# One constant in an expert stage: the order with late combinations lasts to the ninth group of experts, where it lasted to the fourth

## The chip, the cores and the metric

The kernel runs on one core of a Trainium2 chip. The metric is the device time of one execution in microseconds (us), the median over the runs. The core's engines are TensorE (PE in the profile, with its weight loads as PEld), VectorE (DVE), ScalarE (ACT), GpSimd (POOL) and SyncE (SP); SP issues nearly all DMAs.

## What is computed

Two transformer blocks in a row over 512 tokens of width 1024: attention and a feed-forward layer, then a gated linear attention and a layer of experts. The change is in the layer of experts. There are 64 experts in 8 groups of 8; each token goes to 2 experts of one group. Cut to what matters:

```python
def hier_moe(h, w_group, w_expert, w1, w3, w2):
    g_sel = jnp.argmax(g_logits, axis=-1)
    ...
    top_p, top_i = lax.top_k(e_prob, MOE_TOPK)
    gates = g_w[:, None] * top_p / jnp.sum(top_p, axis=-1, keepdims=True)
    ...
    def expert_block(args):
        xb, e = args
        hid = jax.nn.silu(xb @ w1[e]) * (xb @ w3[e])
        return hid @ w2[e]
    ys = lax.map(expert_block, (xs, block_e)).reshape(n_slots, dm)
    ys = ys * slot_gate[:, None].astype(ys.dtype)
    out = jnp.zeros((n_tok + 1, dm), ys.dtype).at[slot_tok].add(ys)[:n_tok]
```

The result is added to the residual and normalized.

## The kernel before, in words

The program is one stream per engine, written out in Python order; nothing reorders it later. After attention, feed-forward and gated linear attention (lines up to about 1000), `experts()` (L1234) does the layer of experts in 16 groups (Q = 16) of four experts, each expert with room for 32 tokens, so that a group is one tile of 128 rows. For group q:

- `choose(q)` (L1252) makes a 0/1 matrix on VectorE, four pairs of operations (L1258, L1260), that says which token sits in which of the 128 rows.
- `gather(half)` (L1263) multiplies it with the tokens on TensorE, 16 products (L1269, 32 records in the trace), and ScalarE copies the result from PSUM in four pieces (L1272). Each half is 512 of the 1024 columns.
- The first products (L1359) multiply the gathered rows with w1 and w3 in two halves (`kind` 0 and 1), each 16 products with 32 columns of weights, 32 records per run in the chain.
- `slots()` (L1274) makes three scalars per row by eight small products (L1280) and a copy on VectorE (L1282).
- ScalarE's SiLU (L1370) and VectorE's product (L1371) give the hidden tile, TensorE transposes it (L1379), ScalarE copies it (L1380).
- `second(q, hs)` (L1293) multiplies with w2 for each half of the columns (L1303); ScalarE scales the result by the gates (L1305), VectorE keeps the remainder (L1308).
- `combine(q, b, hs)` (L1285) sends the rows back to their tokens with two products (L1287, L1288) into a PSUM bank, and VectorE adds it to the accumulator (L1289). `combine_all` does this for four blocks of tokens and two halves: 16 products and 8 adds. The banks are of the tile name `mm`, three of them, which the first products use too.

The order of these steps depends on LEAD (L1329), compared with q at each place. For q <= LEAD, here groups 0 to 3, TensorE's order is: first products of half 0; gather(1) of the same group; first products of half 1; slots; the combinations of group q-1 (`after_slots`, L1339, called at L1373 behind the hidden product, with choose(q+1) ahead of the combinations on VectorE); transposes; second products; gather(0) of the next group. For q > LEAD it is: first products of half 0; slots, with choose(q+1) on VectorE (L1368); first products of half 1; transposes; gather(0) and gather(1) of the next group (L1389, L1390); second products; the combinations of group q itself (L1402). Group LEAD itself does both: the early order, and at its end gather(0), gather(1) and its own combinations. Group 15 has an ending of its own (L1403 and on), with `last_start` (L1425), the final norm and the output.

The weights come through a ring of 20 tiles of 1024 KB in SBUF, made of several pools (`ring_tile`, L1218); twelve tiles serve a group: four for each half of w1 and w3, four for w2. `ring_load` (L1175) issues loads on SP's queue in the order of use: four behind each half of the first products and four behind the second products of every group. A load waits until the products that read the slot's former tile are done; SP's queue is in order, so the loads behind it wait as well. The ring is filled ahead of the stage.

Of the kernel before, what the change touches and what calls it, by code (L numbers as in the profile page):

```python
# [97 lines left out]
class Net:  # L98
# [1135 lines left out]
    def experts(self):  # L1234
# [17 lines left out]
        def choose(q):  # L1252

            s0, s1 = (later[:, q // per - 1, x] if q >= per else self.slot[x] for x in range(2))
            at = iota[:, q % per * P:(q % per + 1) * P]
            for b in range(NB + 1):
                if b < NB:
                    nc.vector.tensor_scalar(oh[:, 0, b], at, s0[:, b:b + 1], None, op0=OP.is_equal)  # L1258
                if b:
                    nc.vector.scalar_tensor_tensor(oh[:, 1, b - 1], at, s1[:, b - 1:b], oh[:, 0, b - 1],  # L1260
                                                   op0=OP.is_equal, op1=OP.add)

        def gather(half):  # L1263

            p = pp.tile([P, NB, P], F32, name="tp", bufs=2)
            k0 = 4 * half
            for b in range(NB):
                for k in range(4):
                    nc.tensor.matmul(p[:, k], self.xt[:, b, (k0 + k) * P:(k0 + k + 1) * P], oh[:, 1, b],  # L1269
                                     start=(b + k == 0), stop=(b == NB - 1), skip_group_check=True)  # L1270
            for k in range(4):
                nc.scalar.activation(xs[:, k0 + k], p[:, k], AF.Copy, scale=self.vec(V_FN2, k0 + k))  # L1272
# [50 lines left out]
        def combine_all(q):  # L1323
            for b in range(NB):
                for hs in halves:
                    combine(q, b, hs)


        LEAD = 3  # L1329
        choose(0)  # L1330
        gather(0)
        next(route)
# [6 lines left out]
        def after_slots(q):  # L1339
            nonlocal tail  # L1340
            if q + 1 < Q:
                choose(q + 1)
            if 0 < q <= LEAD:
                combine_all(q - 1)
            if q + 1 == Q:
                self.last_start()
                tail = start_tail()

        tail = None
        for q in range(Q):  # L1350
            ps = pp.tile([P, 2 * EF], F32, name="mm", bufs=3)
            for kind in range(2):
                if kind and q <= LEAD:
                    gather(1)
# [7 lines left out]
                self.ring_load(4 if q or not kind else 3)  # L1362
                if kind == (q <= LEAD):
                    if q:
                        sv = slots()
                    sc, sg, st = (sv[:, c:c + 1] for c in range(3))
                    if q > LEAD:
                        after_slots(q)  # L1368
            hid = self.rp.tile([P, EF], F32, name="tmp")
            nc.scalar.activation(hid, ps[:, :EF], AF.Silu, scale=sc)  # L1370
            nc.vector.scalar_tensor_tensor(hid, ps[:, EF:], sc, hid, op0=OP.mult, op1=OP.mult)  # L1371
            if q <= LEAD:
                after_slots(q)  # L1373
# [12 lines left out]
            if q + 1 == Q:  # L1386
                break
            if q > LEAD:
                gather(0)  # L1389
# [241 lines left out]
```

## Time and profile before

| what | us |
|---|---|
| median of 3 runs (1430.21 to 1431.56) | 1430.35 |
| the profiled execution, its own time | 1429.98 |
| its span, first to last instruction | 1428.3 |
| busy in the span: PE / PEld | 1354.5 / 1020.4 |
| busy in the span: DVE / ACT / POOL | 739.4 / 542.7 / 118.9 |
| mean granted clock of TensorE | 0.987 |

How to read it: times of the trace are counted from the span's start. "Busy" is the time in which an engine had an instruction under way. The granted clock is 1.00 at 2.4 GHz and 0.50 at 1.2 GHz. In the page's 40 slices each slice is 35.7 us; a digit is a share in tenths, and GB/s is what the DMAs moved. In the chain of waits a line is start, length and what the chain ran through. In a list of waits a line is who waited, "<-" for what, us in total, times, and (where it stands) the longest. In a table of stretches the columns are: from and to; length; busy us (and instructions) of PE, PEld, DVE, ACT and POOL; granted clock; share of the DMA engines' time; GB/s. In the order of time a line is start, length, engine, line, operation, output and inputs, and in square brackets the idle time before it and what ended it. Lines of TensorE's products and weight loads name their output and inputs by tile: `mm`, `tp`, `py` are PSUM, `h` is the pool's name for the gathered rows, the 0/1 matrix and the scaled output.

### The profile page before, as it was taken

Reading aid. Unit: us, or ns where it says so; the run is one execution under the profiler, and the core shown is the slowest. Engines: PE = TensorE matmul, PEld = TensorE weight load, DVE = VectorE, ACT = ScalarE, POOL = GpSimd, SP = SyncE. Lnnn points to the kernel's source line nnn. Section 1 sums busy time; section 2 is a strip of 40 time slices with the busy share of each in tenths; the row PEclk is TensorE's granted clock in tenths of the full one; section 3 lists DMA queues with packets and bytes.
Section 4 is the critical chain, followed back from the end, with each engine's and each line's share of the span. In section 5 each row is a group of like instructions: output and inputs, shape, how many; then the busy total and the mean of one; then the engine's idle time right before and its main releaser. Section 6 shows DMA issues by size and latency. Waiting matters only on the chain.

```text
span 1428.3 us, 20196 instructions
## 1 busy us (share of the span) xinstructions
PE 1354.5 (95%) x8266; PEld 1020.4 (71%) x8266; DVE 739.4 (52%) x1321; ACT 542.7 (38%) x980; POOL 118.9 (8%) x111
## 2 busy tenths in 40 slices
PE   7899999999999999999999999999889999999985
PEld 6688888887888888888887888875456556556542
DVE  6877788775554433444555675552332432432423
ACT  6666666764423212233443354422112112111114
POOL 2101111101100000000322122000000000000001
PEclk9999999999999999999999999999989999999997
DMA  4111111113332322232222123798998999999994
GB/s 181 32 59 60 60 60 60 60 60 120 117 108 89 118 89 89 90 116 89 89 89 79 69 90 117 285 388 323 412 407 357 420 420 421 420 419 421 420 420 179
DMA packets 42495, 282.22 MB, mean 198 GB/s; under 512 B 4864, under 2 KB 5120, under 8 KB 9504
## 3 DMA queue, kind: packets, MB, share of 16 engines
q1 hardware_dynamic: 41616, 280.05, 49.6%
q8 instruction: 66, 1.08, 0.3%
q10 hardware_dynamic: 784, 0.85, 0.2%
q14 instruction: 29, 0.24, 0.0%
HBM read 278.72 MB, written 2.10 MB: 197 GB/s over the span
## 4 chain that ended last, share of the span: by engine, by line
PE 82%; DVE 8%; ACT 4%; DMA 3%; POOL 1%; issue 1%; ACTq 0%; SPq 0%; POOLq 0%; DVEq 0%
PE mm L205 22%; PE mm L331 9%; PE tp L1269 8%; PE py L205 8%; PE tp L205 8%; PE mm L1359 7%; PE py L1303 4%; DMA wring<-in_w_dram 3%; PE mm L773 2%; PE mm L1287 2%; PE tp L1280 2%; PE mm L1288 2%; PE plog L529 1%; POOL sql L392 1%; DVE whl L178 1%
## 5 line engine op out<-in xcount | busy, mean ns | idle before, releaser
L178 DVE TENSOR_TENSOR whl<-wraw,whl 128x1024 fp32r<-128x1024 f32 x138 | 180.9, 1311 | 97.7 <-ACT whl L168 97.4
L168 ACT ACTIVATE whl<-wraw 128x1024 fp32r<-128x1024 f32 x138 | 144.5, 1050 | 102.1 <-PE mm L205 44.2
L331 PE MATMUL mm<-xh,whl 128*128 128x264 f32 (+1 forms) x736 | 181.8, 331 | 0.6 <-DVE whl L178 0.6
L205 PE MATMUL mm<-xh,whl 128*128 128x512 f32 x544 | 175.9, 397 | 0.0
L331 PEld LDWEIGHTS mm<-xh,whl 128*128 128x128 f32 x736 | 119.8, 189 | 15.1 <-issue 3.4
L1269 PEld LDWEIGHTS tp<-h,xt 128*128 128x128 f32 x1024 | 115.9, 192 | 7.8 <-issue 3.4
L1269 PE MATMUL tp<-h,xt 128*128 128x128 f32 x1024 | 118.5, 276 | 0.3 <-DVE h L1260 0.3
L205 PEld LDWEIGHTS mm<-xh,whl 128*128 128x128 f32 x544 | 102.2, 188 | 23.2 <-issue 2.3
L205 PE MATMUL mm<-xl,whl 128*128 128x512 f32 x272 | 106.0, 390 | 0.0
L331 PE MATMUL mm<-xl,whl 128*128 128x264 f32 (+1 forms) x368 | 99.5, 323 | 0.0
L1359 PE MATMUL mm<-wring,h 128*32 128x512 f32 x664 | 96.1, 595 | 3.4 <-ACT h L1272 2.0
L1308 DVE SCALAR_TENSOR_TENSOR h<-py,sv,h 128x512 fp32r<-128x512 f32 (+1 forms) x33 | 24.2, 735 | 137.0 <-ACT h L1305 136.9
L205 PE MATMUL mm<-ogh,whl 128*128 128x512 f32 x256 | 83.6, 396 | 1.5 <-ACT ogh L536 1.5
L1289 DVE TENSOR_TENSOR acc<-acc,mm 128x512 f32<-128x512 f32 (+1 forms) x120 | 73.8, 673 | 8.0 <-PE mm L1288 7.7
L1272 ACT ACTIVATE h<-tp,vecs 128x128 f32<-128x128 f32 x128 | 36.5, 368 | 104.9 <-PE tp L1269 104.9
L1370 ACT ACTIVATE tmp<-mm,sv 128x256 f32<-128x256 f32 x16 | 7.6, 474 | 178.7 <-PE mm L1359 163.6
L1287 PE MATMUL mm<-h,ss 128*128 128x512 f32 (+1 forms) x128 | 61.7, 483 | 9.0 <-DVE acc L1289 5.2
L205 PE MATMUL py<-xh,whl 128*128 128x512 f32 x208 | 65.8, 391 | 0.0
L205 PE MATMUL tp<-xh,whl 128*128 128x512 f32 x208 | 65.2, 389 | 0.0
L331 PEld LDWEIGHTS mm<-xl,whl 128*128 128x128 f32 x368 | 61.8, 189 | 3.2
L616 POOL TENSOR_TENSOR ss<-ss,sq 128x512 f32<-128x512 f32 x21 | 29.2, 1402 | 403.0 <-ACT sq L612 403.0
L205 PEld LDWEIGHTS mm<-xl,whl 128*128 128x128 f32 x272 | 51.1, 188 | 11.5 <-issue 1.4
(420 smaller groups left out, 2540.8 us busy)
## 6 DMA issues: line engine op xcount, KB each, us to landing
wring<-in_w_dram SPq DMA_DIRECT2D x120, 1024.0 KB, 19.8
wraw<-in_wd_dram SPq DMA_DIRECT2D x69, 1024.0 KB, 4.8
whl<-in_w_dram SPq DMA_DIRECT2D x27, 1024.0 KB, 16.1
v<-in_w_dram SPq DMA_DIRECT2D x20, 1024.0 KB, 17.8
wraw<-in_w_dram SPq DMA_DIRECT2D x18, 1024.0 KB, 19.8
h<-in_xT_dram SPq DMA_DIRECT2D x8, 256.0 KB, 5.7
acc<-in_w_dram SPq DMA_DIRECT2D x2, 1024.0 KB
wring<-in_w_dram SPq DMA_DIRECT2D x4, 512.0 KB, 16.9
```

What stands on the lines that cost most here:

```text
L168: self.nc.scalar.activation(hl[:, 0], raw, AF.Copy)
L178: self.nc.vector.tensor_sub(hl[:, 1], raw, hl[:, 0].bitcast(F32))
L205: self.nc.tensor.matmul(out, w, x[:, first + k], start=(at + k == 0 and e == 0), stop=(at + k == of - 1 and e == 2))
L331: nc.tensor.matmul(p[:rows, :m], w[:, wi, k], xx[:, k, o:o + m], start=(n == 0), stop=(n == 3 * KT - 1))
L616: nc.gpsimd.tensor_add(ss, ss, sq)
L773: nc.tensor.matmul(pv[b], x[:, k, bs], w2[:, wi, k % 2], start=(k == 0 and e == 0), stop=(k == KT - 1 and e == 2))
L1269: nc.tensor.matmul(p[:, k], self.xt[:, b, (k0 + k) * P:(k0 + k + 1) * P], oh[:, 1, b], start=(b + k == 0), stop=(b == NB - 1), skip_group_ ...
L1272: nc.scalar.activation(xs[:, k0 + k], p[:, k], AF.Copy, scale=self.vec(V_FN2, k0 + k))
L1287: nc.tensor.matmul(pc, gt[:, b * P:(b + 1) * P], yh[:, hs], start=True, stop=False)
L1289: nc.vector.tensor_add(acc[b][:, hs], acc[b][:, hs] if q else self.xt[:, b, hs], pc)
L1303: nc.tensor.matmul(out, hT[:, e, js], w, start=(e == 0), stop=(e == 1))
L1359: nc.tensor.matmul(ps[32 * j:32 * j + 32], xs[:, kind * 4 + k, 32 * j:32 * j + 32], self.ring[kind, 4 * q + j][:, k * T:(k + 1) * T], star ...
```

## The change

The constant goes from 3 to 8. Groups 4 to 8 then have the order that groups 0 to 3 had (gather(1) between the halves, the combinations of the group before behind the hidden product), and group 8 is the one that also does its own combinations and both gathers at its end. Nothing else is edited; each step's instructions are the same.

```diff
@@ -1326,7 +1326,7 @@
                     combine(q, b, hs)
 
 
-        LEAD = 3
+        LEAD = 8
         choose(0)
         gather(0)
         next(route)
```

## Rows read from the trace of the kernel before

**Rows 1.** The page, 40 slices: TensorE's busy tenths, and GB/s of the DMAs.

```profile
PE   7899999999999999999999999999889999999985
...
GB/s 181 32 59 60 60 60 60 60 60 120 117 108 89 118 89 89 90 116 89 89 89 79 69 90 117 285 388 323 412 407 357 420 420 421 420 419 421 420 420 179
```

**Rows 2.** The chain of waits, expert stage: starts of first (L1359) and second products.

```profile
989.53 3.64 PE mm L1359 x32
...
1018.49 3.64 PE mm L1359 x32
...
1041.18 3.64 PE py L1303 x32
...
1049.11 3.64 PE mm L1359 x32
...
1087.34 3.57 PE mm L1359 x32
...
1131.99 3.69 PE py L1303 x32
...
1302.50 3.57 PE mm L1359 x32
...
1386.22 3.57 PE mm L1359 x32
```

**Rows 3.** Stretches from one group's start to the next: groups 1, 2 and 5.

```profile
989.53:1018.49 28.96, 25.45 (x194) 14.63 (x194) 9.16 (x21) 4.52 (x13) 0.00 (x0) 1.00 0.99 402
1018.49:1049.11 30.62, 27.25 (x194) 16.45 (x194) 9.61 (x21) 4.51 (x13) 0.00 (x0) 0.89 1.00 408
...
1114.19:1141.10 26.91, 25.14 (x199) 14.60 (x202) 9.24 (x22) 4.51 (x12) 0.00 (x0) 1.00 1.01 419
```

**Rows 4.** Weight loads of TensorE in order of time, group 14's second half.

```profile
1362.38 0.14 PEld L1359 LDWEIGHTS mm<-wring,h 128*32 128x32 f32 x2 [0.43 <-DMA wring<-in_w_dram]
1364.86 0.16 PEld L1359 LDWEIGHTS mm<-wring,h 128*32 128x32 f32 x8 [2.34 <-DMA wring<-in_w_dram]
```

**Rows 5.** List of TensorE's waits, 1087 to 1390 (groups 4 to 14).

```profile
PE tp L1379 <- DVE tmp L1371: 12.9, 11, 1.2
PE mm L1288 <- DVE h L1308: 3.2, 11, 0.3
PE mm L1287 <- ACT h L1305: 3.0, 11, 0.3
PE mm L1359 <- DMA wring<-in_w_dram: 1.4, 1, 1.4
```

**Rows 6.** List of TensorE's waits, 980 to 1087 (groups 1 to 3).

```profile
PE mm L1287 <- DVE acc L1289: 4.6, 3, 1.7
PE mm L1359 <- ACT h L1272: 3.3, 6, 0.8
PE py L1303 <- ACT eo L1380: 2.1, 4, 0.5
...
PE mm L1287 <- DVE tmp L1371: 0.7, 3, 0.2
```

**Rows 7.** Stretches of low clock in groups 2, 3 and 15.

```profile
1033.65:1040.45 6.80, 5.25 (x14) 3.58 (x12) 6.02 (x14) 0.00 (x0) 0.00 (x0) 0.50 1.01 422
1064.35:1071.15 6.80, 5.41 (x13) 3.60 (x13) 6.08 (x14) 0.00 (x0) 0.00 (x0) 0.50 1.02 424
1392.05:1398.85 6.80, 6.10 (x10) 3.54 (x11) 1.43 (x8) 1.19 (x2) 0.00 (x0) 0.50 1.02 404
```

**Rows 8.** VectorE and TensorE in order of time, group 2's combinations.

```profile
1032.68 0.48 DVE L1371 SCALAR_TENSOR_TENSOR tmp<-mm,sv,tmp 128x256 f32<-128x256 f32 x1 [0.54 <-ACT tmp L1370]
...
1034.91 2.68 DVE L1289 TENSOR_TENSOR acc<-acc,mm 128x512 f32<-128x512 f32 x4
...
1035.65 0.79 PE L1287 MATMUL mm<-h,ss 128*128 128x512 f32 x1 [1.55 <-DVE acc L1289]
```

**Rows 9.** DMA rate from 1395 to 1410 in 40 slices of 0.375 us.

```profile
GB/s 382 393 437 371 415 404 393 382 421 361 371 333 328 344 333 350 333 317 268 366 317 273 262 197 158 44 27 22 16 0 0 0 0 0 0 0 0 0 0 0
```

## The prediction, made before the changed kernel ran

> **What bounds the kernel now.** I read the page first for the regime. In its 40 slices TensorE is busy 9 tenths nearly throughout, and from slice 31 on the loads run at about 420 GB/s [rows 1]. So two things are near their limit in the expert stage, and the question is which of them ends it. The chain of waits over the stage answers that by the start of each group of four experts, since its first products (L1359, a run of 32) stand on the chain: group 1 starts at 989.53, group 2 at 1018.49, group 3 at 1049.11, group 4 at 1087.34, group 12 at 1302.50 and group 15 at 1386.22 [rows 2]. Groups 0 to 3 are in the order with late combinations ("early groups" from here), groups 4 to 14 in the other ("late groups"). The reader should see three periods in these starts:
>
> - early: 1018.49 to 1049.11 is 30.62 us, the group before it 28.96 us;
> - late: (1302.50 - 1087.34) / 8 = 26.90 us, eight times in a row;
> - the group of the turnover, 3, which does its own and its predecessor's combinations and gathers both halves for its successor: 38.23 us.
>
> A late group uses 12 tiles of 1024 KB, 12.58 MB. At the 419 GB/s of such a stretch [rows 3] this takes 30.0 us, so late groups consume faster (26.90) than the loads deliver, and live on the ring of 20 tiles that the early groups left full. Where does that run out? Groups 12 to 14 take 1386.22 - 1302.50 = 83.72 us where three undisturbed ones take 80.69: 3.03 us in all. The rows of the weight loads on TensorE show the place, group 14's second half: waits of 0.43 and 2.34 us for a DMA at 1362.38 and 1364.86 [rows 4]. Over the eleven late groups the list of waits has only this for the loads [rows 5]. So until 1362 the stage is bound by TensorE's own order of work, and by the loads for 3 us only.
>
> **Why an early group is longer.** Both kinds issue the same instructions, so what differs is what lies between them. In late groups TensorE waits for the hidden product (12.9 us over 11 groups, 1.17 each), and for the two halves of the scaled output (3.2 and 3.0, 0.28 each) [rows 5]: 1.7 us per group. In the early stretch it waits for a bank that the accumulating add must release (4.6 us in three groups, 1.5 each), for the copies of gathered rows (3.3 in six waits, two per group, 1.1), for the transposed hidden tile (2.1 in four, 0.5 each) and shortly for the hidden product (0.7 in three, 0.2 each) [rows 6]: 3.3 us, some 1.6 more. The busy time at full clock is 25.45 against 25.14 [rows 3], 0.3 more. Together 1.9: 26.90 + 1.9 is within 0.2 of group 1's 28.96.
>
> The other 1.66 us, by which group 2 is longer than group 1, is TensorE's clock. It stands at 0.50 (1.2 GHz) for 6.8 us from 1033.65 and again from 1064.35 [rows 7], 15.2 us into groups 2 and 3, where group 1 has 1.00 throughout [rows 3]. What comes just before the fall is a thin stretch: the small products of the slots, four combination products, then the wait for the add. That wait has its reason on VectorE [rows 8]: the hidden product at 1032.68, then the eight operations that choose the next group's rows, and only at 1034.91 the adds, so the next combination (L1287) starts 1.55 us late.
>
> **The change part by part.**
>
> 1. Removed and added: nothing is computed more or less. The number of products, adds, copies and loads is the same; groups 4 to 8 change from the late to the early order.
>
> 2. Groups 4 to 8 become early. The combinations of group q-1 (16 products, 8 adds) move into the wait of group q for its hidden product, so they hide 1.17 us there; the choosing moves from beside the second half's products to ahead of these adds; the gathers no longer lie between the transposes and the second products, so the copies from PSUM stand uncovered. Net price per group 30.62 - 26.90 = 3.72 us. Of the two early periods I take 30.62, not 28.96: both groups that follow another early group with combinations behind them fall in clock, at the same place in the group, and groups 4 to 8 follow such groups. Five of them: 18.6 us.
>
> 3. The turnover moves from group 3 to group 8. Its excess, 38.23 - 30.62 = 7.6 us, is paid once before and once after: nothing. Group 3 becomes a plain early group and group 8 pays.
>
> 4. SP's queue issues the same 12 loads per group at the same places. In an early group the tiles of the second half and of w2 come free later (second products start at 1041.18, 22.7 us after the start; in the late one that starts at 1114.19 they do at 1131.99, 17.8 us [rows 2, 3]), so loads are issued later: at 30.62 us per group against 30.0 of the loads, SP waits for TensorE, and the loads lose 0.6 us per group, 3.1 us in all. They landed by 1406, where the rate falls to nothing [rows 9]; that would be about 1409. The work that reads them is 15 us later by the other terms, so this is hidden by that lag. Without that cover it would show as the 3.03 us did. VectorE's, ScalarE's and GpSimd's queues get the same work per group; nothing else is queued behind the adds but the one-hot of the gates, which stands there in the old early groups as well.
>
> 5. The wait for the loads goes. With six late groups left instead of eleven, TensorE gains 6 x 3.1 = 18.6 us on the loads, where it took ten groups (31 us) to run into them. So the 3.03 us in group 14 disappear: -3.0 us. What is late next is TensorE itself, to the end.
>
> 6. The last group: the clock falls there too, 0.50 from 1392.05 to 1398.85 [rows 7]. Whether it falls again, 15 us later, no row shows. Work done in 6.8 us at half clock takes 3.4 at full; between 0 and -3.4 I take 0, as what precedes it (slots, then a wait for the diagonal) is unchanged, and keep 3 either way for the range.
>
> **Sum:** 18.6 + 0 - 3.0 + 0 = +15.6 us. The profiled execution took 1429.98 us with a span of 1428.3; the median of the runs is 1430.35, 0.4 above it. So 1446.0 us (span 1443.9). A measurement of this kernel tells some 0.2%, 2.9 us, from no change.
>
> **Rivals.**
>
> *The clock stays up in the added groups.* The price per group is then 28.96 - 26.90 = 2.06: 10.3 - 3.0 = +7.3, 1437.6 us. For it: group 1 had the same waits at clock 1.00. Against it: two of two later ones fell. 0.16.
>
> *The loads set the end (not slower).* TensorE's extra 18.6 us would only use up time in which it would otherwise wait for tiles; the end is the last landing plus a fixed tail, and the time stays at 1430.4. This decides if the late groups of the old kernel had waited 16 us or more for loads; they waited 3.0 [rows 4]. For it: the loads' share of 1.01 and the rate of 419 GB/s in a late group [rows 3]. Against it: the ring of 20 tiles, which lets these loads run at full rate without anybody waiting. 0.04. The Trainium skill (Perfetto Trace Analysis, Identifying the Most-Contended Engine) takes the engine with the highest occupancy, or for DMA the bandwidth utilization, as the one to optimize; by that rule the loads bind here and the order of products changes nothing. The trace disagrees as far as the 3.0 us go.
>
> *The clock falls twice in an early group.* A second fall costs up to another 1.66 per group: +8.3, 1454.3 us. For it: five waits per early group instead of three. Against it: the clock was back at 1.00 in the rest of groups 2 and 3 (mean 0.89 over the group [rows 3], which is one fall of 6.8 us). 0.06.
>
> That the change does nothing is excluded by the code: the bound is compared with q at each of the places that decide the order.
>
> **How the numbers follow.** The forecast, early groups at 30.62 with the last group as it was or 3 us off, has 0.72; its own range is 1443 to 1449. The clock staying up 0.16, the loads 0.04, two falls 0.06, and 0.02 for what I don't see. The range goes down to 1437 to take in the first rival and up to 1450 for the last group (3 us) and early groups 0.2 us longer than the one period that I take; left out are the loads, the double fall and the rest. Faster by over 0.2% needs early groups shorter than late ones, which no row shows: 0.01. Within 0.2% holds the loads' case: 0.04. Slower: 0.95.
>
> **What would show it.** In the changed kernel's chain, groups 3 to 8 should start about 30.6 us apart up to a turnover of about 38 in group 8; group 9 should start near 1240, group 15 near 1402. The clock should stand at 0.50 once, 15 us into each of groups 2 to 8. TensorE should have no wait for a load after group 8, and the loads should end near 1409 with the last group still to do. The forecast is wrong if group 9 starts before 1233 (clock up), if TensorE waits for loads in groups 13 to 15 (the loads bind), or if an early group is over 31.5 us.

## The result, and the profile after

The changed kernel takes 1444.56 us (median of 4 runs, 1442.24 to 1445.75) where the kernel before, run beside it, takes 1430.74 (1430.21 to 1431.56): slower, ratio 1.0086 with a 95% interval of 1.0069 to 1.0104, or 13.8 us. Measured once more, beside other runs of the kernel before, it took 1444.31 against 1431.52, ratio 1.0089 (1.0063 to 1.0115). The forecast was 1446.0 within 1437 to 1450.

The profiled execution took 1445.75 us with a span of 1444.0. Its chain of waits gives the starts of the groups, as [rows 2] did before:

```profile
994.06 3.64 PE mm L1359 x32
...
1023.00 3.64 PE mm L1359 x32
...
1053.40 3.64 PE mm L1359 x32
...
1175.96 3.64 PE mm L1359 x32
...
1205.92 3.64 PE mm L1359 x32
...
1242.30 3.57 PE mm L1359 x32
...
1403.52 3.57 PE mm L1359 x32
```

These are groups 1, 2, 3, 7, 8, 9 and 15. Groups 3 to 8, from 1053.40 to 1242.30, take 188.90 us; before, the same six took 38.23 + 5 x 26.90 = 172.7 [rows 2]. The six late groups that are left take 161.22, or 26.87 each. The stretches from one group's start to the next, groups 2, 6, 7, 8 and 10, with the columns of [rows 3]:

```profile
1023.00:1053.40 30.40, 27.38 (x194) 16.57 (x194) 9.60 (x21) 4.52 (x13) 0.00 (x0) 0.89 1.00 413
...
1145.29:1175.96 30.67, 27.21 (x194) 16.45 (x194) 9.60 (x21) 4.52 (x13) 0.00 (x0) 0.89 1.01 413
1175.96:1205.92 29.96, 26.45 (x194) 15.35 (x195) 9.33 (x21) 4.52 (x13) 0.00 (x0) 0.94 1.00 415
1205.92:1242.30 36.38, 33.40 (x246) 20.74 (x250) 13.02 (x28) 6.39 (x19) 0.00 (x0) 1.00 1.01 422
...
1269.15:1296.05 26.90, 25.14 (x198) 14.60 (x202) 9.22 (x22) 4.57 (x12) 0.00 (x0) 1.00 1.01 419
```

The reader should look at the clock (third column from the right): 0.89 in groups 2 to 6, as before in group 2, but 0.94 in group 7 and 1.00 in group 8. The list of TensorE's waits from 980 to 1405 answers to [rows 5, 6]:

```profile
PE mm L1287 <- DVE acc L1289: 12.1, 8, 1.7
PE mm L1359 <- ACT h L1272: 8.5, 16, 0.8
PE tp L1379 <- DVE tmp L1371: 8.3, 7, 1.2
PE py L1303 <- ACT eo L1380: 4.7, 9, 0.5
```

The wait for the first add is there in eight groups, 1.5 us each, and no row of this list, nor of that of the weight loads, names a DMA: the wait for loads of [rows 4] is gone. The loads now end well ahead of their use. The DMA rate from 1390 to 1420 in 40 slices of 0.75 us falls to nothing at about 1410, while the first use of the last w2 tiles is at 1420.96. Before, the loads landed by 1406 [rows 9] and the first use was at 1405.16; those tiles come in three pieces, so the products could start on the first, with hardly anything to spare. After:

```profile
GB/s 371 459 393 459 415 415 426 393 442 410 393 399 415 410 415 396 404 404 377 382 388 391 344 273 158 25 19 0 0 0 0 0 0 0 0 0 0 0 0 0
```

### The profile page after: what moved, and what is told of

It reads as the page before. It is cut to its first block, busy times and chain, and to the rows that moved or that the text cites. A ratio compares the mean times of both kernels' runs of the same rounds, so it can differ in the third digit from the quotient of the medians.

```text
span 1444.0 us, 20196 instructions
## 1 busy us (share of the span) xinstructions
PE 1363.9 (94%) x8266; PEld 1028.2 (71%) x8266; DVE 740.4 (51%) x1321; ACT 543.2 (38%) x980; POOL 118.9 (8%) x111
## 4 chain that ended last, share of the span: by engine, by line
PE 84%; DVE 8%; ACT 4%; POOL 1%; issue 1%; DMA 1%; ACTq 0%; SPq 0%; POOLq 0%; DVEq 0%
PE mm L205 21%; PE mm L331 9%; PE tp L1269 8%; PE mm L1359 8%; PE py L205 7%; PE tp L205 7%; PE py L1303 4%; PE mm L1287 2%; PE mm L773 2%; PE tp L1280 2%; PE mm L1288 2%; PE plog L529 1%; POOL sql L392 1%; PE tp L517 1%; DVE whl L178 1%
## 5 line engine op out<-in xcount | busy, mean ns | idle before, releaser
L1269 PEld LDWEIGHTS tp<-h,xt 128*128 128x128 f32 x1024 | 116.2, 192 | 16.2 <-issue 7.5
L1359 PE MATMUL mm<-wring,h 128*32 128x512 f32 x664 | 94.5, 595 | 5.1 <-ACT h L1272 5.1
L1287 PE MATMUL mm<-h,ss 128*128 128x512 f32 (+1 forms) x128 | 65.5, 512 | 16.2 <-DVE acc L1289 12.7
L331 PEld LDWEIGHTS mm<-xl,whl 128*128 128x128 f32 x368 | 62.2, 191 | 3.2
L1287 PEld LDWEIGHTS mm<-h,ss 128*128 128x128 f32 x128 | 27.7, 217 | 48.0 <-DVE acc L1289 29.5
## 6 DMA issues: line engine op xcount, KB each, us to landing
whl<-in_w_dram SPq DMA_DIRECT2D x27, 1024.0 KB, 12.8
```

The source lines that it names most:

```text
L331: nc.tensor.matmul(p[:rows, :m], w[:, wi, k], xx[:, k, o:o + m], start=(n == 0), stop=(n == 3 * KT - 1))
L1287: nc.tensor.matmul(pc, gt[:, b * P:(b + 1) * P], yh[:, hs], start=True, stop=False)
L1359: nc.tensor.matmul(ps[32 * j:32 * j + 32], xs[:, kind * 4 + k, 32 * j:32 * j + 32], self.ring[kind, 4 * q + j][:, k * T:(k + 1) * T], star ...
```

## The experiments

Theory A picks one entry from the prediction's list of waits: an early group is longer because TensorE waits for the first add, which stands behind the choosing on VectorE, and because the clock falls at that wait; the loads cover the first 3 us of it. Theory B puts the price into the order of the products itself, with copies that nothing covers, which the prediction's part 2 names as well. Each "before" below was measured beside the experiment.

### Where is a group free? One early group fewer

```diff
-        LEAD = 3
+        LEAD = 2
```

> The kernel before with the bound 2 in place of 3: one early group fewer. Theory A with the loads as the limit behind it: TensorE comes 3.7 us earlier to group 4 and waits that much longer for loads in groups 11 to 14 (6 us or more where it waited 3.0), so the time is that of before within 1.5 us (1429.5 to 1431.5). Theory of a fixed price per early group: 13.8 us for five groups is 2.8 each, so 1428.0, and with the rows' 3.7 us 1427.0, with no longer wait for loads.

Measured: 1430.83 us against 1430.02, ratio 1.0007 (0.9997 to 1.0016), no difference that can be told. The late groups, from 1058.70 to 1387.59, take 328.89 us, 6.1 more than twelve at 26.90 would. Half of the waiting is now a group earlier, in group 13 (the first and last line are the starts of groups 3 and 15 in the chain of waits, the two between are weight loads):

```profile
1058.70 3.57 PE mm L1359 x32
...
1333.90 0.14 PEld L1359 LDWEIGHTS mm<-whl,h 128*32 128x32 f32 x2 [0.43 <-DMA whl<-in_w_dram]
1336.39 0.11 PEld L1359 LDWEIGHTS mm<-v,h 128*32 128x32 f32 x1 [2.35 <-DMA v<-in_w_dram]
...
1387.59 3.57 PE mm L1359 x32
```

So most of what TensorE saved in one early group it waited for loads later: from group 1's start to group 15's it took 395.90 us, where the kernel before took 396.69. The price per early group is not a constant: from the bound 2 to 3 it is nothing that the times can tell.

### What does the next group cost once that cover is gone? Four more

```diff
-        LEAD = 3
+        LEAD = 12
```

> The bound 12: four more early groups than in the changed kernel. Theory A: with the bound 8 TensorE no longer waits for loads, so nothing covers further early groups, and each costs its whole price, 2.06 us (clock up) to 3.7 us (clock down), by the changed kernel's own groups 3.2 on the mean: 13 us more than the changed kernel, about 1457 (1452 to 1460), no wait for loads. Theory of a price that the loads partly cover in every group: 1448 to 1451, with a wait for loads in the last groups.

Measured: 1457.97 us against 1431.52, ratio 1.0178 (1.0153 to 1.0203), and 13.7 over the changed kernel's 1444.31 measured beside it, 3.4 per group. TensorE's list of waits has no DMA in it. This is the whole price. Its groups 8, 9 and 11 show how the clock takes part:

```profile
1206.60:1236.57 29.97, 26.46 (x195) 15.34 (x195) 9.34 (x21) 4.52 (x13) 0.00 (x0) 0.94 1.01 417
1236.57:1265.53 28.96, 25.45 (x195) 14.63 (x195) 9.16 (x21) 4.52 (x13) 0.00 (x0) 1.00 1.02 422
1295.64:1326.21 30.57, 27.30 (x195) 16.45 (x195) 9.61 (x21) 4.52 (x13) 0.00 (x0) 0.89 1.01 419
```

In the same order of work, with the same waits, the fall is short in group 8, absent in group 9 and whole in group 11, and the period follows it: 29.97, 28.96, 30.57.

### The clock alone

```diff
-        def combine_all(q):
-            for b in range(NB):
-                for hs in halves:
-                    combine(q, b, hs)
+        def combine_all(q, warm=0):
+            for n, (b, hs) in enumerate((b, hs) for b in range(NB) for hs in halves):
+                if warm and n == 3:
+                    p = pp.tile([P, T], F32, name="tp", bufs=2)
+                    for _ in range(warm):
+                        nc.tensor.matmul(p, self.ident, iota, start=True, stop=True)
+                combine(q, b, hs)
...
-        LEAD = 3
+        LEAD = 8
...
-                combine_all(q - 1)
+                combine_all(q - 1, 2)
```

> The changed kernel (bound 8), with two products of 128x512 that nobody reads put on TensorE between the third and the fourth pair of combination products of an early group, where it waits for the first add. They compute nothing of the result. Theory A: the products fit into the wait of 1.5 us (about 0.2 us over), the clock stays at 1.00 in groups 2 to 7, and the period falls from 30.6 to about 29.2 us: about 8 us less than the changed kernel, near 1436. Theory B, or if the clock's fall costs nothing because the adds set the pace anyway: the period stays at 30.4 us or more, time 1444 to 1447.

Measured: 1436.01 us against 1430.02, ratio 1.0038 (1.0024 to 1.0052): 8.6 under the changed kernel's 1444.56, though that was not measured beside it; against the kernel before, +6.0 where the changed kernel had +13.8. In order of time, TensorE at the place of the wait in one early group; L1328 is the added pair, and it fills the wait:

```profile
1095.20 0.39 PE L1288 MATMUL mm<-h,ss 128*128 128x512 f32 x1
1095.43 1.88 PE L1328 MATMUL tp<-iota,ident 128*128 128x512 f32 x4
1097.29 0.50 PE L1287 MATMUL mm<-h,ss 128*128 128x512 f32 x1
```

Between the second products of neighbouring groups, with the clock in the third column from the right:

```profile
1072.21:1101.16 28.95, 27.14 (x198) 15.39 (x198) 9.15 (x22) 4.51 (x12) 0.00 (x0) 1.00 1.01 421
```

28.95 us is the period of [rows 3]'s group 1, the one at full clock. So the clock's fall is worth 30.6 - 28.95 = 1.65 us per group, and it comes from what TensorE does there: in groups 3 to 7 useless work in the gap removes it. Theory B's 30.4 us or more did not come. Group 2 of this run is the exception, with a period of 30.11. The clock fell there for some 3 us just as the added products began:

```profile
1035.00:1036.00 1.00, 0.76 (x4) 0.45 (x3) 1.00 (x4) 0.00 (x0) 0.00 (x0) 1.00 1.03 426
1036.00:1037.00 1.00, 1.00 (x4) 0.38 (x3) 1.00 (x6) 0.00 (x0) 0.00 (x0) 0.50 1.00 418
```

TensorE was busy through that second microsecond, so here the fall came without the wait: the slots' small products and the first combinations ahead of it have a part in it, and no run separates them from the wait.

### The wait for the add

```diff
         def after_slots(q):
             nonlocal tail
-            if q + 1 < Q:
-                choose(q + 1)
             if 0 < q <= LEAD:
                 combine_all(q - 1)
+            if q + 1 < Q:
+                choose(q + 1)
             if q + 1 == Q:
...
-        LEAD = 3
+        LEAD = 8
```

> The changed kernel (bound 8), with the choosing of the next group's rows put behind the eight adds on VectorE in the early groups. Theory A (an early group is longer by TensorE's wait for the first add, which the choosing delays, and by the fall of the clock behind that wait): the wait of 1.5 us per group goes and the clock stays at 1.00, so the early period falls from 30.6 to about 27.4 us, and the time from 1444.6 to about 1425 to 1430, where the loads (30.0 us per group) begin to bind. If the clock falls all the same: period 29.1, time about 1433. Theory B (the order of the products itself is the price: copies from PSUM that nothing covers): the period stays over 30 us and the time within 3 us of 1444.6.

Measured: 1425.25 us against 1430.02, ratio 0.9968 (0.9956 to 0.9981). VectorE and TensorE in order of time, group 2, answer to [rows 8]:

```profile
1032.42 0.48 DVE L1371 SCALAR_TENSOR_TENSOR tmp<-mm,sv,tmp 128x256 f32<-128x256 f32 x1 [0.55 <-ACT tmp L1370]
1032.82 4.86 DVE L1289 TENSOR_TENSOR acc<-acc,mm 128x512 f32<-128x512 f32 x8
...
1033.55 0.50 PE L1287 MATMUL mm<-h,ss 128*128 128x512 f32 x1
...
1037.60 0.48 DVE L1258 TENSOR_SCALAR h<-iota,slot 128x128 f32<-128x128 f32 x2
```

The adds follow the hidden product at once, the fourth combination (1033.55) has no wait in its row, and the choosing comes 4.8 us later; TensorE's list of waits names no wait for it. An early and a late group of this kernel:

```profile
1018.23:1045.35 27.12, 25.31 (x194) 14.63 (x194) 9.16 (x21) 4.52 (x13) 0.00 (x0) 1.00 1.01 421
...
1242.64:1269.54 26.90, 25.13 (x198) 14.60 (x202) 9.24 (x22) 4.57 (x12) 0.00 (x0) 1.00 1.01 420
```

27.12 against 26.90: of the 3.7 us by which an early group was longer, 1.65 is the clock, 28.95 - 27.12 = 1.83 the add behind the choosing, and 0.22 all that is left for the order of the products. Theory B is out, but for that 0.22.

### The same edit with other bounds

With the choosing behind the adds and the bound of the kernel before, and with the bound 12:

> The kernel before (bound 3), with the choosing put behind the adds in its early groups 1 to 3. Theory A: groups 1 to 3 get 1.5 to 3.2 us shorter each, 7 to 8 us together; TensorE then waits longer for loads in the late groups, so that of these only what the loads themselves gain comes through: they lost time to SP's waits in the early stretch, about 1 us per group and 5 us at the turnover. Time 1425 to 1429, wait for loads over 6 us. Theory B: no change, 1430.7 within 1 us, wait for loads 3.0 us as before.

> The bound 12 with the choosing behind the adds. Theory A: without the wait for the first add the early order costs 27.1 us per group against 26.9 for the late one, so four more such groups cost under 1 us on TensorE, and less where it waits for loads: 1424 to 1427, like the same edit with the bounds 3 and 8. Theory B (some price lies in the order itself): 4 groups times 1 us or more, 1429 and over.

Measured: 1423.75 us against 1430.02 with the bound 3, ratio 0.9952 (0.9936 to 0.9969); 1425.05 against 1431.52 with 12, ratio 0.9952 (0.9936 to 0.9967). Both are faster than the kernel before and than the changed one, and with the bound 8 above they overlap. The stretch from group 1's start to group 15's start says why the bound no longer matters. First the kernel before and the changed one:

```profile
989.53:1386.22 396.69, 366.31 (x2768) 215.22 (x2772) 133.84 (x301) 65.04 (x175) 0.00 (x0) 0.98 1.00 412
```

```profile
994.06:1403.52 409.46, 372.64 (x2768) 220.82 (x2772) 134.89 (x301) 65.22 (x175) 0.00 (x0) 0.95 1.00 412
```

Then the choosing behind the adds with the bounds 3, 8 and 12:

```profile
993.39:1383.52 390.13, 363.16 (x2768) 210.96 (x2772) 132.93 (x301) 65.18 (x175) 0.00 (x0) 1.00 1.01 420
```

```profile
991.10:1381.26 390.16, 363.88 (x2768) 211.14 (x2772) 132.57 (x301) 65.23 (x175) 0.00 (x0) 1.00 1.01 420
```

```profile
991.78:1381.90 390.12, 364.34 (x2768) 211.66 (x2772) 132.24 (x301) 65.04 (x175) 0.00 (x0) 1.00 1.01 420
```

Three kernels with 3, 8 and 12 early groups agree within 0.04 us, at 420 GB/s in the mean over the whole stretch, and in each of them TensorE waits for loads in its last groups: 5.2 us with the bound 3 (301.07 from group 4 to 15, less eleven at 26.90), 4.0 with 8, some 3 with 12. That is the loads' own time. The expectation for the bound 3 had the mechanism and missed three numbers: groups 1 to 3 became 8.8 us shorter together (89.06 where they took 97.81), not 7 to 8; the waits for loads are 5.2 us, not over 6; and 1423.75 lies under its 1425 to 1429.

### The changed kernel once more

> The changed kernel as it is, once more, beside the two others on the same chip. 1442 to 1446, ratio 1.009 within 0.002. What differs between its executions by some us should lie ahead of the expert stage (its first group started 4.5 us later in the profiled execution than in the one of before) and in whether the clock falls in each early group (it did in groups 2 to 6, late in 7, not in 8).

The ratio is given above. Its groups 3 to 6 have 30.80, 30.60, 30.67 and 30.67 us. Groups 7 and 8:

```profile
1173.60:1203.57 29.97, 26.46 (x194) 15.35 (x194) 9.34 (x21) 4.52 (x13) 0.00 (x0) 0.94 1.01 416
1203.57:1239.95 36.38, 33.39 (x246) 20.74 (x250) 13.03 (x28) 6.39 (x19) 0.00 (x0) 1.00 1.01 421
```

The late fall in group 7 and the missing one in group 8 come again in the second profiled execution. From group 1's start to group 15's it takes 409.84 us, where the first took 409.46, although its group 1 starts at 991.33 and not at 994.06: what differs lies ahead of that stretch, as expected.

## Why the prediction was right, point by point

The sign, the size and the mechanism held. That the span agrees to 0.1 us (1444.0, forecast 1443.9) is luck: the terms were 4.3 us too large together, and a late start of the stage, 4.5 us, made up for it. What the terms measured, in the profiled execution:

- **Part 2, five groups that become early: forecast 18.6, measured 188.90 - 172.7 = 16.2.** The step that was too large is the one that took 30.62 us, one fall of the clock, for each of them. It held for groups 3 to 6 (30.55 to 30.71). Group 7 had a shorter fall (29.96) and group 8 none, which is also why its turnover took 36.38 and not 38.23 (part 3). The prediction listed the waits correctly and gave the clock 1.66 us, where the run with filled gaps measured 1.65. (It counts four products of the combinations ahead of the wait; the trace has six, three combinations. Nothing hangs on it.)
- **Why an early group is longer:** the list of waits was set against the late one's, 1.6 us more and 0.3 busy. The runs name the one entry that matters: the add behind the choosing, 1.83. The uncovered copies of part 2 are there, 8.5 and 4.7 us in the list after, but what the combinations hide in their place is worth as much to within 0.22.
- **Part 5, the loads' wait: forecast -3.0.** Six late groups take 161.22 where the six before group 15 took 1386.22 - 1221.80 = 164.42; no DMA is left in the waits. Right, and the run with the bound 2 shows the other side of it.
- **Part 4, the loads:** they ended near 1410, forecast 1409, but in a stage that began 4.5 us late. Counted from group 1's start they took about 416 us, as before, so the 3.1 us that the added groups were to cost them did not come. The added groups did load more slowly (413 GB/s in group 6, 419 in a late one [rows 3]), but behind the turnover less was lost (364 GB/s in group 9; before, 348 in group 4). Either way it is behind the cover that was named.
- **Part 6, the last group: taken as 0.** From its start to the second half's products it took 1415.28 - 1403.52 = 11.76 us, before 1399.47 - 1386.22 = 13.25. The clock fell there for a shorter time. With the choosing behind the adds it did not fall, and the same stretch took 10.24; but it took 10.24 with the bound 12 and the choosing ahead of the adds as well, so that is not the edit's doing. Within the 3 us kept for it.
- **What no part had:** the stage began at 994.06, before at 989.53. Up to there the instructions are the same; the attention's first weight load of L529 starts between 69.0 and 73.7 us in the nine profiled executions of this study, with 69.0, the earliest, in the one of before, and 73.5 and 70.9 in the two of the changed kernel. That is scatter at the start of a run. Terms of the change alone, 16.2 - 3.2 - 1.5 with -0.2 in groups 1 and 2, give 11.3 us of these two executions; the medians say 13.8 and 12.8. What makes up the rest no single execution can show; that the one profiled before started earliest points at the same scatter.

Of the rivals, the clock staying up came true in group 8 and in part in group 7. The loads did not set the end of the changed kernel. They do once the wait for the add is gone, with three orders at 390.1 us. The Trainium skill (Perfetto Trace Analysis, Identifying the Most-Contended Engine) says to optimize the engine with the highest occupancy first, and to take HBM utilization in its place for DMA. The trace agrees with that for these three orders, and not for the step from 3 to 8: there the loads' rate over the stretch was 412 GB/s in both kernels, and the stretch became 12.8 us longer. What differed was whether TensorE waited for a load: 3.0 us before, not at all after.

## What to carry to other kernels

When a step between two dependent engines costs more than its instructions, look at the queue of the engine that must answer: here eight operations that nobody needed yet stood ahead of the add that freed a bank, and moving them behind it took 6.3 us off the kernel before and left 0.22 us per group between the two orders. A stage with a prefetch ring has two prices for the same delay, nothing while the other side would have waited anyway and the full amount after, so measure a step on both sides of that point before a slope is drawn. And once three different orders take the same time to a few hundredths of a microsecond, the order is no longer the limit.

## What was not expected of the hardware

TensorE's clock fell to 0.50 for 6.8 us [rows 7] at a thin stretch whose longest single wait was 1.7 us, and useless products in that wait kept it up in groups 3 to 7, though not in group 2, where it fell as they began. With the same thin stretch in every early group it nevertheless fell some 15 us into group 2, almost 19 us into group 7 and not at all in group 8, in both profiled executions of the changed kernel, and in the run with the bound 12 it was missing in group 9 and came back in groups 10 and 11. What decides that was not tried.
